# The weights of three-tile granules at fourteen column offsets in their rooms

## The chip, the cores and the metric

The kernel runs on one core of a Trainium2 chip. The metric is the device time of one execution in microseconds (us). The kernel before takes 1895.11 us, the median of three runs (1895.04 to 1895.54). One further execution was taken by the hardware profiler; it took 1894.54 us, of which the span from the first to the last instruction is 1892.8 us. "L12" is line 12 of the kernel before.

## The reference, cut to what matters

The program computes two layers of a decoder trunk on 1024 tokens of width 1024, all in float32. The first layer mixes tokens with a short gated convolution, the second with sliding-window attention; after each comes a SwiGLU channel mixer. The change touches the last product of the channel mixer alone, the product with `w_down` ("the down product").

```python
def swiglu_ffn(h, w_gate_up, w_down):
    gu = h @ w_gate_up
    g, u = jnp.split(gu, 2, axis=-1)
    return (jax.nn.silu(g) * u) @ w_down

for i in range(DEPTH):                       # DEPTH = 2
    h = rmsnorm(x, norm_mixer[i])
    x = x + mixer(h)                         # convolution, then attention
    h = rmsnorm(x, norm_ffn[i])
    x = x + swiglu_ffn(h, ffn_w_gate_up[i], ffn_w_down[i])
```

Here `w_down` has 2816 rows (22 blocks of 128) and 1024 columns (8 blocks of 128).

## The kernel before, in words

**Precision.** A float32 factor is kept as two parts, a rounded one ("hi") and the remainder ("lo"). A product is three matmuls: hi x hi, hi x lo, lo x hi. In the code these are L946, L947 and L948, in that order, and each loads its own 128 x 128 stationary block (weights) and streams 512 columns (activations, half of the tokens).

**Seven products for eight.** The large products are computed on 2 x 2 blocks with seven products of sums and differences in place of eight (`KINDS = 7`). The 22 row blocks of `w_down` make `PAIRS = 11` pairs, and the 8 output blocks make `GROUP = 4` units of two. So the down product of a layer is 7 kinds x 4 units, each a sum over 11 tiles of 128 x 128 weights.

**Granules and rooms.** `down_product` (L1388) cuts the 11 tiles of one kind and unit into granules of 4, 4 and 3 tiles. For each granule `ring_granule` (L952) plans three steps:

- `load_raw` (L916): a DMA brings the raw weights, 128 x 512 (or 128 x 384 for three tiles), into a slot `WR` or `WH`, in turn. It is planned 20 us before the granule's first matmul.
- `split_granule` (L922), planned `LEAD = 13.0` us before the first matmul: it takes a *room* from a ring of eight (`G0` to `G7`), a tile of 128 x 2 x 512 float32 values. ScalarE casts the raw weights into the first half of the room (hi, L881), and VectorE subtracts and writes the remainder into the second half (lo, L882).
- `granule_work` (L934): three matmuls for each tile, which read the columns `e * 128` to `e * 128 + 128` of both halves for tile `e`. After the last one the room goes back to the ring.

A granule of four tiles fills each half of its room. A granule of three tiles uses columns 0 to 383 of 512 and leaves 128 columns empty. Each layer has 28 such granules, one for each kind and unit.

**Order.** All engines' instructions are written out in an order that a planner makes: `Line.work` appends matmuls and counts 0.2265 us for each, `at(t, f)` puts every other step at a planned time, and `run` emits them in order of time. An engine carries out its instructions in that order and waits where a semaphore says so. The down product of the first layer runs from about 770 to 945 us of the span, that of the second to the end of the kernel.

The very last product of the kernel (kind 6 of unit 3 of the second layer) has its last tile cut into two halves of 256 columns, so that the output can leave earlier.

Of the kernel before, what the change touches and what calls it, by code (L numbers as in the profile page):

```python
# [15 lines left out]
P = 128  # L16
# [54 lines left out]
def trunk_kernel(ctx: ExitStack, tc: tile.TileContext, xT, small, table, w_in, w_out, w_kv, w_q, w_o, w_gu, w_dn, out):  # L71
# [7 lines left out]
    def slot(tag, shape=(P, D), dtype=F32, bufs=1):  # L79
        uid[0] += 1  # L80
        return sb.tile(list(shape), dtype, tag=tag, name=f"{tag}_{uid[0]}", bufs=bufs)
# [19 lines left out]
    def bank(tag):  # L101
        uid[0] += 1
        if tag == "acc":
            tag = acc_tags[0]
            acc_tags.rotate(-1)
        if tag in ("acc0", "acc1"):
            return ends["pool"].tile([P, 512], F32, tag=tag, name=f"{tag}_{uid[0]}", bufs=1)
        return pm.tile([P, 512], F32, tag=tag, name=f"{tag}_{uid[0]}", bufs=1)

    def plain(ap):  # L110
        return ap.bitcast(F32)
# [125 lines left out]
    state = {}  # L237
# [89 lines left out]
    def conv_layer():  # L327
# [81 lines left out]
        at(-7.6, mean)  # L409
        at(-5.0, turn)  # L410
        tools = scheme(line, ["G0", "G3", "G6", "G7", "G1", "G2", "G4", "G5"])
        units, bank_at, ring_granule = tools.units, tools.bank_at, tools.ring_granule
        B, put = operands_of(
# [374 lines left out]
    class Line:  # L788
# [8 lines left out]
        def at(self, t, f, *args):  # L797
            self.n += 1
            heapq.heappush(self.heap, (t, self.n, f, args))
# [79 lines left out]
    def split_steps(out_hi, out_lo, raw, lo_eng=dve):  # L879
        return (  # L880
            lambda: act.copy(out_hi, raw),  # L881
            lambda: lo_eng.tensor_tensor(out_lo, raw, plain(out_hi), ALU.subtract),  # L882
        )

    def scheme(line, ring_tags):

        at = line.at
        units = {}


        def rooms(tags):

            out_ = []
            for tag in tags:
                if tag in ("WH", "WL"):
                    out_.append(lambda tag=tag: (slot(tag, (P, 2, 4 * P), F32R, bufs=2), tag))
                    continue
                kept = {}

                def one(i, tag=tag, kept=kept):  # L900
                    if not kept:
                        kept[0] = slot(tag, (P, 2, 2, 4 * P), F32R)
                    return kept[0][:, i], tag

                out_ += [lambda i=i, one=one: one(i) for i in (0, 1)]
            return out_

        ring = deque(ring_tags)

        def ring_room():  # L910
            tag = ring.popleft()
            return slot(tag, (P, 2, 4 * P), F32R), tag

        raws = {"n": 0}

        def load_raw(it, src, n):  # L916
            raw = slot(("WR", "WH")[raws["n"] % 2], (P, 4 * P), bufs=2)[:, 0 : n * P]
            raws["n"] += 1
            nc.sync.dma_start(raw, src)
            it["raw"] = raw  # L920

        def split_granule(it, raw_of, n, room, t, lo_eng=dve):  # L922
            def hi():
                w, it["tag"] = room()
                it["w"] = w
                raw = raw_of()
                it["steps"] = split_steps(w[:, 0, 0 : n * P], w[:, 1, 0 : n * P], raw, lo_eng)
                it["steps"][0]()

            at(t, hi)  # L930
            at(t + 0.8, lambda: it["steps"][1]())


        def granule_work(it, n, ops_of, j, bank_of, start, stop, cut=1):  # L934
            for e in range(n):
                last = stop and e == n - 1

                def three(e=e, last=last):
                    w = it["w"]
                    x = ops_of()[(j + e) // 2][:, (j + e) % 2]  # L940
                    ps = bank_of()
                    c = slice(e * P, (e + 1) * P)
                    parts = cut if last else 1
                    for i in range(parts):
                        q = slice(i * HALF // parts, (i + 1) * HALF // parts)
                        pe.matmul(ps[:, q], w[:, 0, c], x[:, 0, q], start=start and e == 0, stop=False, skip_group_check=True)  # L946
                        pe.matmul(ps[:, q], w[:, 0, c], x[:, 1, q], start=False, stop=False, skip_group_check=True)  # L947
                        pe.matmul(ps[:, q], w[:, 1, c], x[:, 0, q], start=False, stop=last, skip_group_check=True)  # L948

                line.work(3, three)  # L950

        def ring_granule(n, ops_of, j, bank_of, start, stop, src=None, raw_of=None, room=None, split=True, lo_eng=dve, cut=1):  # L952

            it = {}
            t = line.end
            if src is not None:
                at(t - LEAD - 7.0, load_raw, it, src, n)
                raw_of = lambda: it["raw"]
            if split:
                split_granule(it, raw_of, n, room or ring_room, t - LEAD, lo_eng)  # L960
            granule_work(it, n, ops_of, j, bank_of, start, stop, cut)
            if split and room is None:
                at(line.end, lambda: ring.append(it["tag"]))
            return it

        def bank_at(u, name, tag):
            def get():
                if (u, name) not in units:
                    units[u, name] = bank(tag)
                return units[u, name]  # L970

            return get

        return SimpleNamespace(
            units=units,
            rooms=rooms,
            ring=ring,
            ring_room=ring_room,
            load_raw=load_raw,
            split_granule=split_granule,  # L980
            granule_work=granule_work,
            ring_granule=ring_granule,
            bank_at=bank_at,
        )
# [20 lines left out]
    def channel_mixer(layer, next_stage, src_of, operands, raw_tags, extra_tags, slots, line, lead_in):  # L1005
# [4 lines left out]
        unit = 12 * MM  # L1010

        tools = scheme(line, [f"G{(3 + i) % RING}" for i in range(RING)])
        units, rooms, ring, ring_room = tools.units, tools.rooms, tools.ring, tools.ring_room
        load_raw, split_granule, granule_work = tools.load_raw, tools.split_granule, tools.granule_work
# [1312 lines left out]
```

## Time and profile before

| What | Before |
|---|---|
| median of three runs | 1895.11 us |
| profiled execution | 1894.54 us |
| its span | 1892.8 us |
| TensorE, matmuls busy | 1887.4 us, 8603 matmuls |
| VectorE busy | 1368.5 us |
| ScalarE busy | 844.4 us |
| GpSimd busy | 319.1 us |
| granted clock of TensorE | 1.000 |

In rows of the profile PE is TensorE's matmuls, PEld its weight loads, DVE VectorE, ACT ScalarE, POOL GpSimd and SP the engine that issues most DMAs. A row of the timeline has the start in us, the duration in us, the engine, the line, the operation, the tile written and the tiles read (without their numbers, so `G0` to `G7` are all `G`), and the shapes. A matmul's record lasts longer than the distance to the next one, because matmuls are pipelined; the distance between two starts is what a matmul costs in a dense stream.

### The profile page before, as it was taken

How to read it: one execution, taken by the hardware profiler on the slowest of the kernel's cores; microseconds unless marked ns; L12 is line 12 of the kernel's file. 1: busy time of each engine (PE TensorE's matmuls, PEld its weight loads, DVE VectorE, ACT ScalarE, POOL GpSimd, SP SyncE). 2: the span in 40 equal slices, each digit the busy share in tenths (PEclk: the TensorE clock that was granted, in tenths of full speed). 3: DMA queues.
4: the chain of work that ended last, by engine and by line, in shares of the span. 5: the costliest groups of instructions: out<-in, count | busy, mean ns of one | idle time of the engine just before them, and what ended most of it. 6: DMA issues, size and time to landing. Idle time of an engine off the chain costs nothing.

```text
span 1892.8 us, 24868 instructions
## 1 busy us (share of the span) xinstructions
PE 1887.4 (100%) x8603; PEld 1569.8 (83%) x8603; DVE 1368.5 (72%) x2224; ACT 844.4 (45%) x1694; POOL 319.1 (17%) x620
## 2 busy tenths in 40 slices
PE   9999999999999999999999999999999999999999
PEld 7888888888888888888888888888888888888887
DVE  8997878868778776666678888567767676765543
ACT  6544444533333334444557776335333333344441
POOL 0000011012122221000015777300111111100000
PEclk9999999999999999999999999999999999999999
DMA  8522176146766656987641115844454654577563
GB/s 315 173 96 78 67 292 219 56 162 225 229 215 219 230 200 237 361 295 249 228 138 30 35 25 170 326 147 145 149 179 160 218 183 156 175 279 263 196 226 102
DMA packets 162558, 352.43 MB, mean 186 GB/s; under 512 B 16192, under 2 KB 62656, under 8 KB 162304
## 3 DMA queue, kind: packets, MB, share of 16 engines
q1 hardware_dynamic: 135936, 257.88, 40.8%
q0 software_dynamic: 26208, 92.81, 13.5%
q8 instruction: 67, 1.10, 0.2%
q14 instruction: 59, 0.48, 0.1%
q10 hardware_dynamic: 288, 0.16, 0.0%
HBM read 241.34 MB, written 103.28 MB: 182 GB/s over the span
## 4 chain that ended last, share of the span: by engine, by line
PE 98%; DVE 1%; issue 0%; DMA 0%; ACT 0%; POOL 0%; DVEq 0%; ACTq 0%
PE acc L946 16%; PE acc L948 16%; PE acc L947 16%; PE P L946 9%; PE P L948 9%; PE P L947 9%; PE P L1654 2%; PE P L1656 2%; PE P L1655 2%; PE acc L1061 2%; PE acc L1062 2%; PE acc L1063 2%; PE twin L1881 2%; PE acc L175 1%; PE acc L1961 1%; PE acc L1930 1%
## 5 line engine op out<-in xcount | busy, mean ns | idle before, releaser
L946 PE MATMUL acc<-XS,G 128*128 128x512 f32 x880 | 342.9, 390 | 0.0
L948 PE MATMUL acc<-XS,G 128*128 128x512 f32 x880 | 342.8, 390 | 0.0
L947 PE MATMUL acc<-XS,G 128*128 128x512 f32 x880 | 342.7, 389 | 0.0
L947 PEld LDWEIGHTS acc<-XS,G 128*128 128x128 f32 x880 | 165.3, 188 | 34.2
L946 PEld LDWEIGHTS acc<-XS,G 128*128 128x128 f32 x880 | 165.3, 188 | 34.2
L948 PEld LDWEIGHTS acc<-XS,G 128*128 128x128 f32 x880 | 165.3, 188 | 34.1
L948 PE MATMUL P<-A,G 128*128 128x512 f32 x476 | 185.4, 389 | 0.0
L946 PE MATMUL P<-A,G 128*128 128x512 f32 x476 | 185.4, 389 | 0.0
L947 PE MATMUL P<-A,G 128*128 128x512 f32 x476 | 185.4, 389 | 0.0
L946 PE MATMUL acc<-A,G 128*128 128x512 f32 x441 | 171.8, 390 | 0.0
L948 PE MATMUL acc<-A,G 128*128 128x512 f32 x441 | 171.6, 389 | 0.0
L947 PE MATMUL acc<-A,G 128*128 128x512 f32 x441 | 171.5, 389 | 0.0
L882 DVE TENSOR_TENSOR G<-WL,G 128x512 fp32r<-128x512 f32 x168 | 117.0, 697 | 47.8 <-ACT G L881 47.8
L881 ACT CAST G<-WR 128x512 fp32r<-128x512 f32 (+1 forms) x200 | 120.8, 605 | 59.9 <-PE acc L948 25.9
L882 DVE TENSOR_TENSOR G<-WR,G 128x512 fp32r<-128x512 f32 (+1 forms) x200 | 133.2, 666 | 9.0 <-ACT G L881 8.6
L881 ACT CAST G<-WH 128x512 fp32r<-128x512 f32 (+1 forms) x158 | 95.0, 601 | 83.0 <-PE acc L948 34.0
L1233 ACT ACTIVATE G<-G 128x512 f32<-128x512 f32 x88 | 55.8, 634 | 159.7 <-DVE G L1304 155.6
L946 PE MATMUL P<-XS,G 128*128 128x512 f32 x316 | 123.2, 390 | 0.1
L947 PE MATMUL P<-XS,G 128*128 128x512 f32 x316 | 123.1, 389 | 0.0
L948 PE MATMUL P<-XS,G 128*128 128x512 f32 x316 | 123.1, 389 | 0.0
L881 ACT CAST G<-WL 128x512 fp32r<-128x512 f32 x168 | 103.6, 617 | 42.5 <-DVE WL L821 38.0
L882 DVE TENSOR_TENSOR G<-WH,G 128x512 fp32r<-128x512 f32 (+1 forms) x158 | 106.6, 675 | 7.9 <-ACT G L881 7.7
(332 smaller groups left out, 3801.4 us busy)
## 6 DMA issues: line engine op xcount, KB each, us to landing
G<-h SPq DMA_DIRECT2D x70, 512.0 KB, 5.1
h<-X POOLq DMA_DIRECT2D x44, 512.0 KB, 5.3
X<-in_w_dn SPq DMA_DIRECT2D x80, 256.0 KB, 3.7
s<-X POOLq DMA_DIRECT2D x40, 512.0 KB, 4.5
WR<-in_w_gu SPq DMA_DIRECT2D x36, 512.0 KB, 5.7
WH<-in_w_gu SPq DMA_DIRECT2D x36, 512.0 KB, 6.2
h<-X POOLq DMA_DIRECT2D x66, 256.0 KB, 3.6
WR<-s SPq DMA_DIRECT2D x54, 256.0 KB, 3.4
```

The source lines that it names most:

```text
L881: lambda: act.copy(out_hi, raw),
L882: lambda: lo_eng.tensor_tensor(out_lo, raw, plain(out_hi), ALU.subtract),
L946: pe.matmul(ps[:, q], w[:, 0, c], x[:, 0, q], start=start and e == 0, stop=False, skip_group_check=True)
L947: pe.matmul(ps[:, q], w[:, 0, c], x[:, 1, q], start=False, stop=False, skip_group_check=True)
L948: pe.matmul(ps[:, q], w[:, 1, c], x[:, 0, q], start=False, stop=last, skip_group_check=True)
L1061: pe.matmul(ps, hi[:, kc], xs[:, 0, c], start=k == 0, stop=False, skip_group_check=True)
L1062: pe.matmul(ps, hi[:, kc], xs[:, 1, c], start=False, stop=False, skip_group_check=True)
L1063: pe.matmul(ps, lo[:, kc], xs[:, 0, c], start=False, stop=k == n_op - 1, skip_group_check=True)
L1233: state["silu"] = act.activation(x, x, AF.Silu)
L1654: pe.matmul(ps, x[:, 0, t], hi, start=k == 0, stop=False)
L1655: pe.matmul(ps, x[:, 0, t], lo, start=False, stop=False)
L1656: pe.matmul(ps, x[:, 1, t], hi, start=False, stop=k == NK - 1)
```

## The change

Granules of three tiles are written at a column offset in both halves of their room, and read there. The offset goes through a list of fourteen, from 0 to 128 columns, in the order in which the granules are split, and begins again after the last. Since each layer has 28 such granules, the list is used twice in each. Granules of four tiles stay as they are. `SKEWS` and the counter stand once in the kernel, ahead of `scheme`, so the count runs on from the first layer to the second.

```diff
+    SKEWS = (0, 4, 8, 12, 16, 24, 32, 40, 48, 64, 80, 96, 112, 128)
+    state["skew"] = 0
+
     def scheme(line, ring_tags):
...
         def split_granule(it, raw_of, n, room, t, lo_eng=dve):
             def hi():
                 w, it["tag"] = room()
-                it["w"] = w
                 raw = raw_of()
-                it["steps"] = split_steps(w[:, 0, 0 : n * P], w[:, 1, 0 : n * P], raw, lo_eng)
+                skew = 0
+                if n == 3:
+                    skew = SKEWS[state["skew"] % len(SKEWS)]
+                    state["skew"] += 1
+                it["w"] = w[:, :, skew : skew + n * P]
+                it["steps"] = split_steps(it["w"][:, 0], it["w"][:, 1], raw, lo_eng)
                 it["steps"][0]()
```

An offset of one column is four bytes of a partition's memory. The matmuls' code is unchanged: it reads columns `e * 128` of `it["w"]`, which now begins at the offset.

## The prediction

> **What bounds the kernel now.** I read the page's head first, then the table of 100 us windows, the waits of TensorE, and the timeline of the stage that the change touches.
>
> ```profile
> span 1892.8 us, 24868 instructions
> PE 1887.4 (100%) x8603; PEld 1569.8 (83%) x8603; DVE 1368.5 (72%) x2224; ACT 844.4 (45%) x1694; POOL 319.1 (17%) x620
> PEclk9999999999999999999999999999999999999999
> PE 98%; DVE 1%; issue 0%; DMA 0%; ACT 0%; POOL 0%; DVEq 0%; ACTq 0%
> ```
>
> TensorE is busy for 1887.4 of 1892.8 us, the granted clock is full in every slice, and the chain of waits that ended last runs through TensorE for 98% of the span. Busy time alone says little, because a matmul's record (0.39 us) overlaps the next one's. So I looked at who kept TensorE waiting, and at the stage itself.
>
> ```profile
> engine line waited for: us in total, times, longest us
> PE P L353 <- DVE s L350: 1.1, 1, 1.1
> PE acc L1930 <- POOL G L1924: 0.2, 1, 0.2
> ```
> ```profile
> 780.00:945.00 165.00, 165.00 (x730) 136.68 (x729) 111.93 (x175) 79.04 (x122) 6.06 (x8) 1.00 0.80 273
> 1710.00:1875.00 165.00, 165.00 (x729) 136.75 (x728) 84.70 (x121) 67.59 (x98) 0.00 (x0) 1.00 0.61 205
> ```
>
> The two windows lie inside the two down products. Columns are TensorE, weight loads, VectorE, ScalarE and GpSimd busy, with counts. TensorE never rests there, and the table of waits names no matmul of lines L946 to L948. The time of this stage is therefore the number of matmuls times the interval from one start to the next. I call that interval the period; it is what the change can move.
>
> The timeline of the first down product, TensorE's rows alone, shows a granule of four tiles and then one of three. A tile is three matmuls, L946, L947 and L948.
>
> ```profile
> 784.38 0.39 PE L946 MATMUL P<-A,G 128*128 128x512 f32 x1
> ...
> 785.06 0.39 PE L946 MATMUL P<-A,G 128*128 128x512 f32 x1
> ...
> 785.74 0.39 PE L946 MATMUL P<-A,G 128*128 128x512 f32 x1
> ...
> 786.42 0.39 PE L946 MATMUL P<-A,G 128*128 128x512 f32 x1
> ...
> 787.10 0.39 PE L946 MATMUL P<-XS,G 128*128 128x512 f32 x1
> 787.33 0.39 PE L947 MATMUL P<-XS,G 128*128 128x512 f32 x1
> ...
> 789.14 0.39 PE L946 MATMUL P<-A,G 128*128 128x512 f32 x1
> ```
>
> The four tiles begin at 784.38, 785.06, 785.74 and 786.42, and the next granule at 787.10: 0.68 us each. By the code their weights stand at columns 0, 128, 256 and 384 of each half of the room. So four column offsets, 128 columns apart, have the same period: (787.10 - 784.38)/12 = 0.2267 us. The three-tile granule from 787.10 to 789.14 has nine matmuls: 2.04/9 = 0.2267 us as well. No offset that isn't a multiple of 128 columns is used by these lines before.
>
> **The change part by part.** Nothing is added to or taken from the program: no instruction, transfer, wait or room. The 56 granules of three tiles (28 a layer: seven kinds times four units, one each) shift by 0, 4, 8, 12, 16, 24, 32, 40, 48, 64, 80, 96, 112 and 128 columns in turn. The list goes round twice in each layer, so each offset gets 4 granules, 36 matmuls of full width. (The very last granule has its last tile cut into two halves; its offset is 128, the last of the list.)
>
> Offset 0 is the old place. Offset 128 puts its three tiles at columns 128, 256 and 384, whose period stands above: nothing new. Twelve offsets remain, 48 granules, 48 x 9 = **432 matmuls** at starts that the trace does not show. Every nanosecond on all of them is 0.432 us; 0.2% of the kernel, 3.8 us, is 8.8 ns on each.
>
> *The stationary read.* First, what there is to gain. In the attention stage eight matmuls of 256 columns run back to back:
>
> ```profile
> 1044.29 1.11 PE L1881 MATMUL twin<-G,G 128*128 128x256 f32 x8
> 1045.24 0.63 PE L1961 MATMUL acc<-G,G 128*128 128x512 f32 x2
> ```
>
> Their period is (1045.24 - 1044.29)/8 = 0.1188 us. Half the columns save 226.7 - 118.8 = 107.9 ns, so 512 columns take 215.8 ns and 10.9 ns of each period is a fixed part that doesn't depend on width. If a good offset did away with all of it at all twelve: 432 x 10.9 = 4.7 us less. That is the lower bound.
>
> In a sentence beside this, the Trainium skill (TensorE: Matmul & The Clock Gate, section "Back-to-back issue gap") gives a single matmul of 512 columns a gap of N/2.4 + 2.5, about 216 ns; the trace has 226.7 ns, and by the page's figure there would be an estimated 432 x 10.9 = 4.7 us to win if the difference came from where the weights lie. The same page ("Step-by-step: what each phase is for") says that weight loads and the moving operand have two independent read ports and don't take bandwidth from each other, by which an offset would win nothing; no run here shows either.
>
> Next, what it could cost. The nearest row where a 512-wide matmul lasts longer is in attention, where other work is on the chip; beside it, for comparison, a row of the lines in question:
>
> ```profile
> L1654 PE MATMUL P<-X,XS 128*128 128x512 f32 x64 | 25.5, 398 | 0.0
> L946 PE MATMUL P<-XS,G 128*128 128x512 f32 x316 | 123.2, 390 | 0.1
> ```
>
> That is 8 ns more (398 against 390), whatever its cause: 432 x 8 = 3.5 us. If an unlucky start doubled the fixed part instead, it would be 432 x 10.9 = 4.7 us more. The upper bound is the larger, 4.7 us.
>
> *The weight load.* It could become longer at an offset. Its cover is the matmul before it. The last six matmuls of the kernel, half as wide, show how much cover that is:
>
> ```profile
> 1888.28 0.19 PEld L948 LDWEIGHTS acc<-A,G 128*128 128x128 f32 x1
> 1888.39 0.28 PE L948 MATMUL acc<-A,G 128*128 128x256 f32 x1
> 1888.39 0.19 PEld L946 LDWEIGHTS acc<-A,G 128*128 128x128 f32 x1
> 1888.51 0.28 PE L946 MATMUL acc<-A,G 128*128 128x256 f32 x1
> ```
>
> Loads of 0.19 us start 0.11 us apart here: they are pipelined, and a new one can go every 0.12 us or sooner. Under a 0.2267 us period a load must take nearly twice as long (0.11 us more) before it sets anything. Below that it costs nothing.
>
> *The split.* ScalarE's cast and VectorE's subtraction write the shifted place.
>
> ```profile
> 784.80 0.51 ACT L881 CAST G<-WH 128x384 fp32r<-128x384 f32 x1 [2.44 <-DMA WH<-in_w_dn]
> 785.60 0.55 DVE L882 TENSOR_TENSOR G<-WH,G 128x384 fp32r<-128x384 f32 x1
> ```
> ```profile
> 794.58 0.39 PE L946 MATMUL P<-XS,G 128*128 128x512 f32 x1
> ```
>
> The sixth three-tile split of the first layer ends at 786.15, and the sixth three-tile granule starts on TensorE at 794.58: 8.4 us of cover. I take it that a shifted write costs what it does now. Were both twice as long, that adds 0.51 + 0.55 us against 8.4 us, and 24 x 0.55 = 13 us of VectorE time per down product, where it is busy for 111.93 and 84.70 of 165 us. Nothing queued behind it comes late enough to reach TensorE. Cost: nothing; were the cover gone, the shifted splits would add 48 x 1.06 = 51 us, the far end of this term, which I leave out for the cover.
>
> *The sum.* Between -4.7 and +4.7 us I take 0 for the read, because four offsets already measured agree to the last digit shown; 0 for the load and 0 for the split. The profiled execution took 1894.54 us, 1.74 us more than its span, and I leave it at **1894.54 us**. That is 0.57 us under the median of the runs, 1895.11, so the forecast in the measure of the runs is **1895.1 us**.
>
> **The rivals.**
>
> *A start off the old steps makes the stationary read collide with the moving one (slower).* Place: the 432 matmuls of L946 to L948. For it speaks that every period the trace has for these lines is at starts 128 columns apart, so a finer rule would have stayed unseen. Against it speaks that four offsets agree to the last digit. If the fixed part doubles at all twelve offsets: 1895.1 + 4.7 = 1899.8 us. It decides from 8.8 ns on each; at five offsets alone (4, 8, 12, 24, 40, those that aren't multiples of 16 columns), 180 matmuls, it needs 21 ns.
>
> *Some weight loads outgrow their cover (slower).* At those same five offsets, a load that occupies three times the 0.118 us above, 0.354 us, would set the period: (354 - 227) x 180 = 23 us, 1918 us. It begins at twice the time: (236 - 227) x 180 = 1.6 us, still not to be told from nothing. Against it: the load's record shows hardly any spread.
>
> ```profile
> L948 PEld LDWEIGHTS P<-A,G x476: 187/188/188, 63.3 to 1873.4; 128*128 128x128 f32 x159
> ```
>
> Here the Trainium skill speaks (SBUF — State Buffer, "Specifications (TRN2)"): lines of memory are 16 bytes, four fp32 values, and crossing into a new one has a price. All fourteen offsets are multiples of four columns, so by that rule each load crosses as many lines as before and this rival does not arise; no run here shows it yet.
>
> *The fixed part is itself a collision that the old steps suffer, and offsets off them escape it (faster).* For it: 10.9 ns that width doesn't explain. Against it: one would have to escape at nearly all twelve, since at half of them it is 216 x 10.9 = 2.4 us, not to be told from nothing. At all of them: 1895.1 - 4.7 = 1890.4 us.
>
> *The change doesn't reach its matmuls* (a granule cut elsewhere than its tiles are read): the matmuls read the same cut that the split writes, so this would show in the numbers and not in time; 1895.1 us, and no chance of its own.
>
> **How the numbers follow.** A measurement of this kernel tells about 0.2%, 3.8 us, from no change. Forecast, no change: 0.74. Collision: 0.13; outgrown loads: 0.04; both count as slower, 0.17. Escape: 0.09, faster. The likeliest case alone spans 1894 to 1897 us, which allows for a few nanoseconds at some offsets. The range takes both bounds of the unknown read, 1890.4 to 1899.8; only outgrown loads, and an offset dearer than a doubled fixed part, lie outside.
>
> **What would show each step.** The windows inside the two down products should hold the same number of matmuls, 730 and 729 give or take one, and the nine matmuls of each three-tile granule should span 2.04 us at every offset. If an offset matters, its four granules (the same place in the list, twice in each layer) show it alike, and the four-tile granules between them don't. The weight load's record should stay at 187 to 188 ns, the cast and the subtraction of 384 columns at 0.51 and 0.55 us. The prediction is wrong if nine matmuls at several offsets take 2.12 us or more, or 1.96 us or less, or if TensorE is seen waiting for L881 or L882.

## The result and the profile after

| | before | changed |
|---|---|---|
| median of 20 runs | 1894.79 us (1894.37 to 1895.54) | 1898.01 us (1897.46 to 1900.21) |
| ratio | | 1.0017, 95% interval 1.0010 to 1.0024 |
| profiled execution | 1894.54 us | 1897.95 us |
| its span | 1892.8 us | 1896.3 us |

The change made the kernel 3.2 us slower, 0.17%. That is small, but clear of the scatter. The head of the page after and the table of TensorE's waits:

```profile
span 1896.3 us, 24868 instructions
PE 1891.0 (100%) x8603; PEld 1569.4 (83%) x8603; DVE 1368.4 (72%) x2224; ACT 843.8 (44%) x1694; POOL 319.3 (17%) x620
```
```profile
PE P L353 <- DVE s L350: 1.1, 1, 1.1
PE acc L1937 <- POOL G L1931: 0.2, 1, 0.2
```

The counts of instructions are the same, and TensorE waits for others where it waited before, for 1.1 and 0.2 us. VectorE and ScalarE work as long as before. Only TensorE's busy time grew, by 3.6 us. In the code after, L946 to L948 have become L953 to L955. The two windows inside the down products:

```profile
780.00:945.00 165.00, 165.00 (x723) 135.62 (x722) 110.27 (x173) 77.53 (x120) 6.06 (x8) 1.00 0.80 273
1710.00:1875.00 165.00, 165.00 (x724) 135.62 (x723) 85.54 (x121) 67.19 (x99) 0.00 (x0) 1.00 0.62 209
```

In the same 165 us there were 730 and 729 matmuls before; now there are 723 and 724. TensorE is still never idle, and the clock is still full (1.00). So matmuls are issued farther apart. (By the starts of its matmuls the first down product runs from 757 to 962 us before, apart from two granules that come earlier, and not from 770 to 945 as said above; both windows lie inside the down products. Its first kind has its four three-tile granules, at the offsets 0, 4, 8 and 12, right behind one another; elsewhere two granules of four tiles follow each granule of three. The second layer does the same.)

The timeline of TensorE shows where. These are the starts of four three-tile granules, at the offsets 16, 32, 64 and 80, each with the first row of the granule behind it:

```profile
787.31 0.40 PE L953 MATMUL P<-XS,G 128*128 128x512 f32 x1
...
789.41 0.39 PE L953 MATMUL P<-A,G 128*128 128x512 f32 x1
...
802.45 0.40 PE L953 MATMUL P<-XS,G 128*128 128x512 f32 x1
802.69 0.40 PE L954 MATMUL P<-XS,G 128*128 128x512 f32 x1
...
804.56 0.40 PE L953 MATMUL P<-A,G 128*128 128x512 f32 x1
...
806.64 0.39 PE L953 MATMUL P<-A,G 128*128 128x512 f32 x1
...
825.13 0.39 PE L953 MATMUL acc<-XS,G 128*128 128x512 f32 x1
...
827.17 0.39 PE L953 MATMUL acc<-A,G 128*128 128x512 f32 x1
...
832.61 0.40 PE L953 MATMUL acc<-XS,G 128*128 128x512 f32 x1
...
834.71 0.39 PE L953 MATMUL acc<-A,G 128*128 128x512 f32 x1
```

Nine matmuls take 2.10 us at offset 16, 2.11 at 32, 2.04 at 64 (as before) and 2.10 at 80. The first interval at offset 32 is 0.24 us in place of 0.2267. And it does not end with the granule: the nine matmuls behind the one at 32, whose weights are not shifted at all, take 806.64 - 804.56 = 2.08 us.

From the starts of all matmuls in the two traces, which are kept to the nanosecond, I worked out the excess of each three-tile granule over the 2040 ns before. "Aftermath" is the excess of the unshifted matmuls behind it. Four granules have each offset, and the two layers agree within 3 ns. (Three granules at 112 and 128 are left out: two have matmuls of the next stage among or behind them, and the kernel's last has the cut tile.)

| offset | 0, 64, 128 | 4 | 8 | 12 | 16, 80 | 24 | 32, 96 | 40 | 48, 112 |
|---|---|---|---|---|---|---|---|---|---|
| nine matmuls, ns over 2040 | 0 | 0 to 9 | 51 to 56 | 54 to 60 | 62 to 63 | 60 | 67 to 68 | 58 | 21 |
| aftermath, ns | 0 | 0 | 0 to 23 | 0 to 22 | 10 to 13 | 38 to 40 | 46 to 48 | 38 to 40 | 0 |

Where the aftermath is 0 at 8, the next granule was itself a shifted one; at 12 it is 0 where the granule ahead was the disturbed one at 8, and 21 or 22 where the granule ahead was not shifted. All of it adds up to 2.97 us. With 0.11 us in the interval ahead of a shifted granule, during which its first weights are loaded, it is 3.08 us: the two down products together. The 3.22 us between the medians are explained but for 0.14. (Elsewhere single executions differ by up to 1.4 us, at the very start and at a stall near 424 to 427 us; the comparisons below use the two down products alone where a trace is read.)

The rows of one weight load and its matmul, with the matmul's row before ahead of them, and of the two steps that write the shifted places:

```profile
L948 PE MATMUL P<-A,G x476: 388/389/390, 63.5 to 1873.7; 128*128 128x512 f32 x159
```
```profile
L955 PEld LDWEIGHTS P<-A,G x476: 187/188/192, 63.2 to 1876.8; 128*128 128x128 f32 x159
L955 PE MATMUL P<-A,G x476: 387/389/402, 63.4 to 1877.0; 128*128 128x512 f32 x159
```
```profile
L882 DVE TENSOR_TENSOR G<-WR,G 128x384 fp32r<-128x384 f32 x12 | 6.6, 551 | 0.0
L881 ACT CAST G<-WR 128x384 fp32r<-128x384 f32 x12 | 6.1, 510 | 5.9 <-PE acc L955 4.2 <-DMA WR<-in_w_dn 1.1 <-ACT G L881 0.4
```

In this group a load takes at most 192 ns in place of 188 before, but a matmul up to 402 in place of 390. The writes take what they took, 551 and 510 ns.

### The profile page after: what moved, and what is told of

It is laid out like the page before. It is cut to its first block, busy times and chain, and to the rows that moved or that the text cites. A ratio compares the mean times of both kernels' runs of the same rounds, so it can differ in the third digit from the quotient of the medians.

```text
span 1896.3 us, 24868 instructions
## 1 busy us (share of the span) xinstructions
PE 1891.0 (100%) x8603; PEld 1569.4 (83%) x8603; DVE 1368.4 (72%) x2224; ACT 843.8 (44%) x1694; POOL 319.3 (17%) x620
## 4 chain that ended last, share of the span: by engine, by line
PE 98%; DVE 1%; issue 0%; ACT 0%; POOL 0%; DMA 0%; DVEq 0%; ACTq 0%
PE acc L953 16%; PE acc L955 16%; PE acc L954 16%; PE P L953 9%; PE P L955 9%; PE P L954 9%; PE P L1661 2%; PE P L1662 2%; PE P L1663 2%; PE acc L1068 2%; PE acc L1070 2%; PE acc L1069 2%; PE twin L1888 2%; PE acc L175 1%; PE acc L1968 1%; PE acc L1937 1%
## 5 line engine op out<-in xcount | busy, mean ns | idle before, releaser
L953 PE MATMUL acc<-XS,G 128*128 128x512 f32 x880 | 342.8, 390 | 0.0
L954 PE MATMUL acc<-XS,G 128*128 128x512 f32 x880 | 342.7, 389 | 0.0
L955 PE MATMUL acc<-XS,G 128*128 128x512 f32 x880 | 342.6, 389 | 0.0
L955 PEld LDWEIGHTS acc<-XS,G 128*128 128x128 f32 x880 | 165.2, 188 | 34.7
L954 PEld LDWEIGHTS acc<-XS,G 128*128 128x128 f32 x880 | 165.2, 188 | 34.6
L953 PEld LDWEIGHTS acc<-XS,G 128*128 128x128 f32 x880 | 165.2, 188 | 34.4
L953 PE MATMUL P<-A,G 128*128 128x512 f32 x476 | 185.4, 390 | 0.0
L954 PE MATMUL P<-A,G 128*128 128x512 f32 x476 | 185.3, 389 | 0.0
L955 PE MATMUL P<-A,G 128*128 128x512 f32 x476 | 185.3, 389 | 0.0
L953 PE MATMUL acc<-A,G 128*128 128x512 f32 x441 | 171.9, 390 | 0.0
L954 PE MATMUL acc<-A,G 128*128 128x512 f32 x441 | 171.6, 389 | 0.0
L955 PE MATMUL acc<-A,G 128*128 128x512 f32 x441 | 171.6, 389 | 0.0
L882 DVE TENSOR_TENSOR G<-WL,G 128x512 fp32r<-128x512 f32 x168 | 117.1, 697 | 48.4 <-ACT G L881 48.4
L881 ACT CAST G<-WR 128x512 fp32r<-128x512 f32 (+1 forms) x200 | 120.8, 605 | 62.9 <-PE acc L955 31.3
L882 DVE TENSOR_TENSOR G<-WR,G 128x512 fp32r<-128x512 f32 (+1 forms) x200 | 133.3, 666 | 9.0 <-ACT G L881 8.6
L881 ACT CAST G<-WH 128x512 fp32r<-128x512 f32 (+1 forms) x158 | 94.9, 601 | 77.3 <-PE acc L955 34.9
L953 PE MATMUL P<-XS,G 128*128 128x512 f32 x316 | 123.3, 390 | 0.1
L954 PE MATMUL P<-XS,G 128*128 128x512 f32 x316 | 123.3, 390 | 0.0
L955 PE MATMUL P<-XS,G 128*128 128x512 f32 x316 | 123.2, 390 | 0.0
L881 ACT CAST G<-WL 128x512 fp32r<-128x512 f32 x168 | 103.6, 617 | 41.9 <-DVE WL L821 37.6
L882 DVE TENSOR_TENSOR G<-WH,G 128x512 fp32r<-128x512 f32 (+1 forms) x158 | 106.5, 674 | 6.8 <-ACT G L881 6.7
```

## The experiments

**All granules at one dear offset.** The list of offsets is cut to one:

```diff
-    SKEWS = (0, 4, 8, 12, 16, 24, 32, 40, 48, 64, 80, 96, 112, 128)
+    SKEWS = (32,)
```

> All 56 three-tile granules at offset 32. In the trace of the changed kernel a granule at 32 costs 54 ns more in its own matmuls, 14 ns at its end and 46 ns in the nine matmuls of the unshifted granule after it, 114 ns in all. Theory (each granule pays for itself and for its aftermath, independent of its neighbours): 56 x 0.114 = 6.4 us more, 1901.2 us. Rival (the aftermath seen there came from the change of offset from granule to granule, not from the offset): 56 x 0.068 = 3.8 us, 1898.6 us.

Measured: 1901.50 us against 1895.22, ratio 1.0034 (1.0021 to 1.0046), 6.3 us more. In the trace the two down products together, with the matmuls right behind them, are 6.00 us longer. The theory said 6.4, its rival 3.8 us. In the window of the second down product there are 718 matmuls in place of 729:

```profile
1710.00:1875.00 165.00, 165.00 (x718) 134.72 (x717) 86.62 (x123) 68.64 (x99) 0.00 (x0) 1.00 0.64 214
```

So the cost stays with the offset, aftermath and all, and is not one of changing it.

**The streams and the weights moved as a whole.** Two kernels without offsets inside the rooms move whole groups of tiles. In the first everything large goes 32 columns down, in the second the streamed operands do while a pad holds the rooms of the granules' weights where they were:

```diff
-C_ROOM = 496
+C_ROOM = 464
...
+    slot("pad", (P, 32))          # the second kernel alone
     for tag in [f"G{k}" for k in range(12) if k != 2]:
```

> The kernel before with every large tile, streamed operands and weights alike, 32 columns lower in memory (the constants' room is 32 columns smaller); no offsets inside rooms. Theory (distance of weights from streamed columns): the distance is unchanged, 1894.8 us, period 226.7 ns. Rival (the weights' own address counts): all 6387 matmuls of the granules lie where offset 32 lies, at 6.7 ns more each (60 ns in nine): 43 us more, about 1938 us.

> The kernel before with the streamed operands, and the slots WR, WH and WL, 32 columns lower in memory, while the rooms of the granules' weights and everything behind them stay where they are. Theory (distance): the 6387 matmuls of the granules are now 32 columns off at 6.7 ns each, 43 us more, about 1938 us. Rival (the weights' own address counts): they haven't moved, 1894.8 us.

Measured, in a single run of each: 1894.58 us for both moved, 1935.73 us for the streams alone, against 1895.22 us. The second down product's window of each, both moved first:

```profile
1710.00:1875.00 165.00, 165.00 (x729) 136.64 (x728) 84.69 (x121) 67.25 (x98) 0.00 (x0) 1.00 0.61 205
```
```profile
1710.00:1875.00 165.00, 165.00 (x709) 132.75 (x708) 89.81 (x126) 67.83 (x101) 2.56 (x4) 1.00 0.69 234
```

729 matmuls in 165 us as before, and 709. The dearest group of the kernel with the streams moved (busy us, then mean ns of one; 390 before), and rows of its timeline:

```profile
L947 PE MATMUL acc<-XS,G 128*128 128x512 f32 x880 | 347.7, 395 | 0.0
```
```profile
801.08 0.40 PE L947 MATMUL P<-A,G 128*128 128x512 f32 x1
801.33 0.40 PE L948 MATMUL P<-A,G 128*128 128x512 f32 x1
801.56 0.39 PE L949 MATMUL P<-A,G 128*128 128x512 f32 x1
...
802.71 0.40 PE L948 MATMUL P<-A,G 128*128 128x512 f32 x1
802.95 0.40 PE L949 MATMUL P<-A,G 128*128 128x512 f32 x1
```

The weights of the second kernel lie at the same addresses as before, and yet it is 40.5 us slower; the theory said 43. So the address of the weights alone does not decide, and by the first kernel that of the streams doesn't either; their distance does. (The raw slots `WR`, `WH` and `WL` move along with the streams. They can't be the cause: in the changed kernel the loss fell in a granule's own matmuls and those behind, some 8 us behind the split that reads these slots.)

The 6386 intervals that begin with one of the three matmul lines took 38.3 us more together, 6.0 ns each on average. In the first layer nearly all of them (3488 of 3612) follow a pattern of seven to within 2 ns: 241, 233, 230, 232, 228, 230, 232 ns, and again from 241; the rows show two of the long ones, at 801.08 and 802.71. The nine matmuls of a granule at 32 in the changed kernel are the same pattern, cut off: 241, 232, 231, 232, 228, 230, 232, 241, 240. In the second layer nearly all (2740 of 2774) follow another pattern, 229 to 230 and 237 to 238 ns in turn, also 32 columns off. Its rows show it in the records, 0.40 and 0.39 us in turn:

```profile
1720.27 0.40 PE L948 MATMUL acc<-A,G 128*128 128x512 f32 x1
1720.50 0.39 PE L949 MATMUL acc<-A,G 128*128 128x512 f32 x1
1720.73 0.40 PE L947 MATMUL acc<-A,G 128*128 128x512 f32 x1
1720.97 0.39 PE L948 MATMUL acc<-A,G 128*128 128x512 f32 x1
```

The first pattern makes 232.4 ns a matmul, the second 233.3. So one distance can have two rhythms, each kept up through most of a layer; what picks between them here is not shown.

**Fourteen other offsets, twice.** The list of offsets alone is replaced, by multiples of one and two among others:

```diff
-    SKEWS = (0, 4, 8, 12, 16, 24, 32, 40, 48, 64, 80, 96, 112, 128)
+    SKEWS = (1, 2, 3, 6, 10, 14, 20, 28, 36, 44, 52, 56, 60, 63)
...
+    SKEWS = (5, 7, 9, 11, 18, 22, 26, 30, 34, 38, 42, 46, 50, 54)   # the second kernel
```

> The change with fourteen other offsets: 1, 2, 3, 6, 10, 14, 20, 28, 36, 44, 52, 56, 60, 63. Read from the trace: the time of nine matmuls for each offset (2040 ns is undisturbed). Theory (distance, repeating every 64 columns, good near 0): 1, 2, 3 about 2040; 6 between 2045 and 2090; 10, 14, 20, 28, 36, 44 between 2090 and 2110; 52 and 56 at most 2060; 60 and 63 2040; none under 2040; the whole about 1897.2 us. Rival 1 (a start must be a multiple of four columns): 1, 2, 3, 6, 10, 14 and 63 dearer than their neighbours among the multiples of four, over 2060 already at 1. Rival 2 (the fixed part can be escaped): some offset under 2030.

> The change with fourteen more offsets: 5, 7, 9, 11, 18, 22, 26, 30, 34, 38, 42, 46, 50, 54. Known so far, in excess of 2040 ns for nine matmuls: 0 at 0, 4, 10, 36, 60, 63; 27 or less at 3; 21 to 24 at 44 and 48; 38 to 49 at 1, 2, 6, 20, 52; 54 to 68 at 8, 12, 14, 16, 24, 28, 32, 40, 56. Theory (the cost is set by the distance alone, but not by how near it is to a multiple of 64 or of four): most of them 20 to 70 ns over, one to four of them free, no order by size; none under 2040. Rival (a simple rule by distance): neighbours of free offsets, 5, 9, 11, 34, 38, are cheap, under 20 ns over, and the rest dear.

Measured, in a single run of each: 1897.76 and 1897.52 us, against 1895.22 and 1895.04; the down products are 2.44 and 3.10 us longer. Nine matmuls, in ns over 2040, all distances known so far taken together:

| | offsets (ns over 2040) |
|---|---|
| free | 0, 4 (9 where the granule behind is at 8, whose first weights are loaded in the last interval), 10, 30, 36, 54, 60, 63 |
| free or dear, by how entered | 3 (0 or 27), 7 (0 or 74), 9 (0 or 72) |
| 20 to 50 | 48 (21), 44 (24), 38 (37), 6 (38), 2 (44), 46 (45), 52 (45), 50 (46), 20 (48), 11 (49), 34 (50) |
| over 50 | 1, 8, 5, 22, 28, 12, 26, 40, 56, 14, 18, 24, 16, 42, 32 (51 up to 68) |

My picture for the first map, good near 0 and dear in the middle, fell: offset 1 costs 49 to 54 ns, 36 nothing. Starting on a multiple of four columns isn't the rule either: 10, 30, 54 and 63 are free. Rows of the first map, the tile starts of two granules, show it at 10 and at 14:

```profile
787.83 0.39 PE L953 MATMUL P<-XS,G 128*128 128x512 f32 x1
788.50 0.39 PE L953 MATMUL P<-XS,G 128*128 128x512 f32 x1
789.18 0.39 PE L953 MATMUL P<-XS,G 128*128 128x512 f32 x1
789.87 0.39 PE L953 MATMUL P<-A,G 128*128 128x512 f32 x1
...
795.32 0.40 PE L953 MATMUL P<-XS,G 128*128 128x512 f32 x1
796.01 0.39 PE L953 MATMUL P<-XS,G 128*128 128x512 f32 x1
796.72 0.40 PE L953 MATMUL P<-XS,G 128*128 128x512 f32 x1
797.41 0.39 PE L953 MATMUL P<-A,G 128*128 128x512 f32 x1
```

2.04 us at offset 10, 2.09 at 14. In the second map, which expected no order, the rival that neighbours of free offsets are cheap fell too (5: 54, 11: 49, 34: 50 ns). Nor does the distance alone set the cost, as both maps' theories had it: at 3, 7 and 9 one and the same distance was free in two granules and dear in two. Of the 64 distances 37 are measured by now; none came under 2040 ns by more than 1 ns, by which undisturbed granules differ too.

**The free offsets alone.**

```diff
-    SKEWS = (0, 4, 8, 12, 16, 24, 32, 40, 48, 64, 80, 96, 112, 128)
+    SKEWS = (10, 36, 60, 63)
```

> The change with the offsets 10, 36, 60 and 63 alone, in turn: all 56 three-tile granules are shifted, none by a multiple of 64 columns. In the map of fourteen other offsets these four left the nine matmuls of a granule at 2040 ns. Theory (the distance alone counts, and these four distances are free): the kernel before, 1894.8 to 1895.3 us, each granule 2040 ns. Rival 1 (a shift costs something at its start and end, or in the split, that the granules' own nine matmuls don't show): at the 3.2 us that the change cost or half of it, 1896.5 to 1898 us. Rival 2 (those offsets were free because of what came ahead of them in that list): granules of 2.06 to 2.11 us, 1897 us or more.

Measured: 1894.80 us against 1895.04, ratio 1.000 (0.999 to 1.001). Every granule is shifted, none by a multiple of 64, and all of the loss is back; each takes 2039 to 2041 ns. Shifting as such costs nothing, neither in the split nor at a granule's edges. Its windows:

```profile
780.00:945.00 165.00, 165.00 (x729) 136.69 (x728) 111.66 (x175) 78.81 (x122) 6.06 (x8) 1.00 0.80 273
1710.00:1875.00 165.00, 165.00 (x730) 136.70 (x729) 85.90 (x123) 67.70 (x98) 0.00 (x0) 1.00 0.62 208
```

**Each map's offsets 64 columns farther.**

```diff
-    SKEWS = (0, 4, 8, 12, 16, 24, 32, 40, 48, 64, 80, 96, 112, 128)
+    SKEWS = (74, 100, 118, 94, 69, 106, 73, 71, 65, 66, 70, 84, 92, 108)
```

> The change with fourteen offsets that are each 64 columns beyond one of the maps': 74, 100, 118, 94 (10, 36, 54, 30 there), 69, 106, 73, 71 (5, 42, 9, 7), 65, 66, 70, 84, 92, 108 (1, 2, 6, 20, 28, 44). Theory (the cost repeats every 64 columns, however irregular it is inside them): nine matmuls take 2040 ns at 74, 100, 118, 94, 73 and 71, which are all entered from undisturbed granules or free ones; 2094 at 69, 2103 at 106, 2094 at 65, 2081 at 66, 2078 at 70, 2088 at 84, 2096 at 92, 2064 at 108, each within 5 ns. Rival (the repeat seen at 16 and 80, 32 and 96, 48 and 112 holds for such round numbers alone): no match at the odd ones.

Measured in a single run, nine matmuls in ns, in the order of the list: 2040, 2040, 2040, 2040, 2094, 2103, 2040, 2040, 2093, 2081, 2078, 2088, 2096, 2064. All fourteen agree with the forecast within 2 ns. The whole took 1896.92 us beside a run of the kernel before of 1895.84, the down products 2.01 us more than before. The rows show 106 and 73:

```profile
795.07 0.40 PE L953 MATMUL P<-XS,G 128*128 128x512 f32 x1
...
797.17 0.39 PE L953 MATMUL P<-A,G 128*128 128x512 f32 x1
...
802.62 0.39 PE L953 MATMUL P<-XS,G 128*128 128x512 f32 x1
...
804.65 0.39 PE L953 MATMUL P<-A,G 128*128 128x512 f32 x1
```

2.10 us at 106, and 2.03 by the two digits of the rows at 73 (2040 ns by the trace's starts). So the cost repeats every 64 columns, 256 bytes of a partition, however ragged it is inside them.

**Offset 9 alone.**

```diff
-    SKEWS = (0, 4, 8, 12, 16, 24, 32, 40, 48, 64, 80, 96, 112, 128)
+    SKEWS = (9,)
```

> All 56 three-tile granules at offset 9. In the second map a granule at 9 took 2040 ns in two cases and 2112 ns in two, where it came straight behind a disturbed granule at 7, itself behind one at 5. Theory (offset 9 has two states, and which one a granule falls into is set by how it is entered): no granule here comes behind a disturbed one, so all take 2040 ns and the kernel 1894.8 to 1895.3 us. Rival (the place in the list or the room decides): some granules of 2.11 us, those that open each down product first.

Measured: all three-tile granules of the down products 2040 ns, the down products within 0.01 us of before, the whole 1895.29 us beside a run of the kernel before of 1895.84. In the second map a granule at 9 behind a disturbed one took 2111 ns. The rows are of the third granule of the first layer, in the second map and then here:

```profile
777.57 0.39 PE L953 MATMUL acc<-XS,G 128*128 128x512 f32 x1
...
779.68 0.40 PE L953 MATMUL acc<-XS,G 128*128 128x512 f32 x1
```
```profile
777.67 0.39 PE L953 MATMUL acc<-XS,G 128*128 128x512 f32 x1
...
779.71 0.39 PE L953 MATMUL acc<-XS,G 128*128 128x512 f32 x1
```

The place in the order and the offset are the same, and it takes 2.11 us there and 2.04 here. So at 9 columns either pace can run, and the granules ahead decide which.

**One half of the weights at 32.** Two kernels, with `SKEWS = (32,)`, shift the lo half alone, and the hi half alone. The three matmul lines, not shown, read `w[0]` and `w[1]` in place of `w[:, 0]` and `w[:, 1]`:

```diff
-                it["w"] = w[:, :, skew : skew + n * P]
-                it["steps"] = split_steps(it["w"][:, 0], it["w"][:, 1], raw, lo_eng)
+                at_hi, at_lo = 0, skew        # the other kernel: skew, 0
+                it["w"] = w[:, 0, at_hi : at_hi + n * P], w[:, 1, at_lo : at_lo + n * P]
+                it["steps"] = split_steps(it["w"][0], it["w"][1], raw, lo_eng)
```

> All three-tile granules with the lo half of the weights at offset 32 and the hi half at 0, so one load of three is off. With both halves at 32 nine matmuls take 2107 ns, 67 more than 2040. Theory 1 (each load pays for itself): a third, about 22 ns, 2062 ns, and the kernel 1/3 of 6.3 us more, 1897.0 us. Theory 2 (what costs is the state in which loads and streams follow each other, and it lasts beyond the load that disturbs it): not a third; anything from 2040 to 2110 ns, and more than one of the three intervals of a tile is longer. If the load under way collides with the stream of the matmul under way, the interval that begins at the second hi matmul (in which lo is loaded) is the first to be longer.

> All three-tile granules with the hi half at offset 32 and the lo half at 0, so two loads of three are off. Theory 1 (each load pays for itself): two thirds of 67 ns, nine matmuls 2085 ns, the kernel 2/3 of 6.3 us more, 1899.0 us. Theory 2 (the state): not two thirds, and this kernel's cost and that of the lo half alone need not add up to the cost of both.

Measured: 1898.16 and 1899.15 us, single runs, against 1895.04; the down products 2.18 and 3.97 us longer. (Of the first kernel's 3.1 us more, 0.9 lies elsewhere, mostly at the very start and at the stall near 425 us.) Nine matmuls take 2079 to 2081 ns with lo off, 2106 to 2109 with hi off in all but the first four granules of a layer, and neither has an aftermath. So nine matmuls are not in thirds: 40 ns and 67 in place of 22 and 45, with 67 for both halves off. But the down products are nearly so: 2.18 and 3.97 us of 6.00. The two theories were not as far apart as I had put them. One load that is off among good ones costs 13 ns (40/3), and nine times that, 120 ns, is what nine in a row cost with the interval ahead (6), their own (67) and their aftermath (47); yet in the unbroken streams above each costs 5.7 or 6.6. What speaks for a state that lasts is where the time appears. Rows of the kernel with lo off, where L954 and L955 multiply by hi and L956 by lo:

```profile
788.66 0.39 PE L954 MATMUL P<-XS,G 128*128 128x512 f32 x1
788.89 0.40 PE L955 MATMUL P<-XS,G 128*128 128x512 f32 x1
789.12 0.40 PE L956 MATMUL P<-XS,G 128*128 128x512 f32 x1
789.36 0.39 PE L954 MATMUL P<-XS,G 128*128 128x512 f32 x1
```

The three intervals are 227, 232 and 234 ns. Lo is loaded while the second hi matmul streams; that interval is the first to grow, and the one behind it, in which well-placed weights are loaded, grows more.

## Why the prediction failed

The forecast was no change, 1895.1 us. The kernel lost 3.2 us, within the stated range and under the 0.2% that I had put as the limit of what can be told. That limit was too coarse: twenty runs told the loss from nothing (0.10 to 0.24%). That the range held is partly luck, because nothing in the runs ties the loss to the doubled fixed part from which its upper bound came. By its steps:

- **What bounds the kernel: right.** The stage is the number of matmuls times the period. The loss is in the period and nowhere else; TensorE waits for nobody new.
- **The value 0 for the stationary read: the step that failed.** I took 0 between -4.7 and +4.7 us "because four offsets already measured agree to the last digit shown". The four lie 128 columns apart, and the runs show that the cost repeats every 64. They were one measurement four times over, and said nothing of the other distances. The same row, read for what it leaves out, should have left the two bounds as open as before. The term measured 2.11 us in the matmuls themselves, 4.9 ns on each of 432, and 0.97 us around them.
- **The rival "collision": right in place and direction, with its size misjudged.** Shifted matmuls of these lines became slower; that the two reads collide is not shown. Its price was the doubled fixed part, 10.9 ns on each; with all that hangs on them the shifted matmuls cost 3.08/0.432 = 7.1 ns each. Its guess at which offsets are dear, those that aren't multiples of 16 columns, was wrong: 32 and 16 are the dearest of the list, and 4 costs next to nothing.
- **No term for what comes behind.** I counted the 432 shifted matmuls and nothing else. 0.86 us lies in the unshifted ones that follow. The sign "the four-tile granules between them don't" show it failed by this.
- **The weight load: its length right, "below that it costs nothing" not.** In the group shown it grew by 4 ns at most where it needed 109, and the "outgrown loads" fell. In its place the matmul's own record grew, by up to 15 ns in the offset-32 granule. With lo off the interval in which the shifted weights are loaded was the first to grow, so a load's place can cost without a longer load.
- **The split: right.** 551 and 510 ns against 550 and 509, and no wait on L881 or L882; the free offsets show it by themselves.
- **The rival "escape": fell.** No distance of 37 tried went under the period of 226.7 ns, so at none of them did placement win back any of the 10.9 ns.
- **The signs.** The windows (723 and 724 matmuls for 730 and 729) and the granules that should have stayed at 2.04 us told that the forecast was wrong. The sign of 2.12 us did not: the dearest granules of the list took 2.108 us.

Of the Trainium skill: the page TensorE: Matmul & The Clock Gate ("Step-by-step: what each phase is for") says that loading the next weights doesn't take bandwidth from the running matmul. By that the place of the weights should not slow the stream; where the weights lay 32 columns off all streams the kernel took 40.5 us more, so the measurement decides. The estimate of 4.7 us to be won, worked out from that page's gap, was not borne out at any distance. The lines of 16 bytes on SBUF — State Buffer ("Specifications (TRN2)") fit the load's own record here, which hardly changed. But in the two maps, with starts that aren't multiples of four columns, no load of these lines took over 193 ns either, the most before, so the record doesn't test them. Nor do they tell dear offsets from free ones: 16 and 36 are both multiples of four columns.

**What stays open.** That a read of the weights and a read of the stream get in each other's way is argued, from the distance rule and from the interval that grows first; no row shows the two meeting. Why distances like 10, 30, 36 and 54 are free and their neighbours not, and why the pace takes up to nine matmuls to recover behind some of them, isn't settled. A loop of loads and streams that delay each other and fall into a repeating pattern would do all of this, two paces and two rhythms at one distance among it, but no run here tells that from another cause.

## What to carry to other kernels

In a dense stream of matmuls like this one, with a load for each, put weights and streamed operands at a distance that is a multiple of 256 bytes in the partition, and check the period from start to start after every change of a tile's size or place, since a pad of 128 bytes in the wrong spot cost this kernel 2%. When agreement of several rows is to carry a zero, ask first whether the rows differ in what the change varies; rows taken at multiples of one step say nothing of what lies between. A term counted only over the instructions that an edit touches leaves out those behind them in the same pipeline.

## What the hardware showed unexpectedly

The period of a 512-column matmul depends on how far the weights lie from the streamed columns: 226.7 ns at multiples of 64 columns; in an unbroken stream at 32 columns 232.4 ns with a rhythm of seven matmuls in the first layer, and 233.3 ns with a rhythm of two in the second. The dependence repeats every 64 columns to within 2 ns over nine matmuls, where it was compared, and is ragged inside. At 3, 7 and 9 columns there are two paces at one and the same distance; at 9 the runs show that the granules ahead pick one. Unshifted matmuls behind a disturbed granule stay slow for up to nine matmuls.
